# Cutting the rows of a kernel's first load into four 1 KB runs: sum of ReLU over the last axis

## The chip, the cores and the metric

One core of a Trainium2 chip; its loads are issued by SyncE (SP), whose queue runs on 16 DMA engines. The metric is the device time in microseconds (us) of one execution, the median of several. All runs quoted here were fast, with a granted clock of 1.0.

## The reference

```python
def setup_inputs():
    batch, seq, dim = 32, 512, 1024
    return {"x": np.random.randn(batch, seq, dim).astype(np.float32)}

def reference(x):
    return np.sum(np.maximum(x, 0), axis=-1).astype(np.float32)
```

16384 rows of 4 KB, 67.1 MB to read, 64 KB to write.

## The kernel before

Each of the 128 partitions takes 112 neighbouring rows of a first region and 16 of a second. The first region comes in seven chunks of 16 rows into three buffers that are used in turn; the second in ever smaller loads, so that little is left to compute when the last bytes land. ScalarE (ACT) applies ReLU in place and VectorE (DVE) sums; towards the end both do both in one instruction with an accumulator.

```python
BIG = 16; NB = 3; D = 1024
CHUNKS = [[(0, 0, 1), (0, 1, 15)]] + [[(0, 16 * c, 16)] for c in range(1, 7)]
# ... (cut)
for c in range(NBIG + 1):
    if c >= NB:
        sp.wait_ge(s_dve, done[c - NB])          # the buffer is free again
    if c < NBIG:
        i = 0
        for g, j, n in CHUNKS[c]:                # region, first row, rows
            sp.dma_start(
                out=buf[:, c % NB, i : i + n, :], in_=xv[g][:, j : j + n, :]
            ).then_inc(s_in[c], 16)
            i += n
            if c == 0:                           # issue ahead of the start barrier
                code.insert(arrival, code.pop())
                arrival += 1
# ... (cut: tail loads; compute; the last store waits for both engines)
```

The first chunk goes as two loads: one row for each partition (512 KB), then the other 15 (7.5 MB). Everything that computes on it waits for both (`s_in[0]` at 32).

## Time and profile before

| | before |
|---|---|
| time, three runs | 160.84, 160.88, 160.95 us |
| span of the profiled execution | 159.5 us |
| packets of the load queue, share of 16 engines | 2448, 98.1% |
| issue of the first load (the instruction on SP that starts it) | 0.000 to 0.383 us |
| first packet starts / last data packet ends | 1.007 / 157.107 us |

A packet is one descriptor's transfer: one contiguous run moved by one of the 16 DMA engines. The trace has start, duration and size of each; where I speak of packet records, I counted in those. "In flight" is the number of packets that have started and not ended, 16 when every engine works on one. The views that carry the argument stand in the prediction below. One line is added here, the first of the chain in order of time (start, duration, what): the issue of the first load.

```profile
0.00 0.38 SPq L91
```

### The profile page before, as it was taken

Reading aid. Unit: us, or ns where it says so; the run is one execution under the profiler, and the core shown is the slowest. Engines: PE = TensorE matmul, PEld = TensorE weight load, DVE = VectorE, ACT = ScalarE, POOL = GpSimd, SP = SyncE. Lnnn points to the kernel's source line nnn. Section 1 sums busy time; section 2 is a strip of 40 time slices with the busy share of each in tenths; the row PEclk is TensorE's granted clock in tenths of the full one; section 3 lists DMA queues with packets and bytes.
Section 4 is the critical chain, followed back from the end, with each engine's and each line's share of the span. In section 5 each row is a group of like instructions: output and inputs, shape, how many; then the busy total and the mean of one; then the engine's idle time right before and its main releaser. Section 6 shows DMA issues by size and latency. Waiting matters only on the chain.

```text
span 159.5 us, 149 instructions
## 1 busy us (share of the span) xinstructions
DVE 120.5 (76%) x59; ACT 101.5 (64%) x54; POOL 0.2 (0%) x4
## 2 busy tenths in 40 slices
DVE  0000000009999999999999999999999999898985
ACT  3000059990699808996099951999329980496975
POOL 0000000000000000000000000000000000000000
DMA  9969996996997998979969969969969979798994
GB/s 378 493 293 447 493 526 263 526 526 263 526 477 312 526 427 362 526 312 477 526 296 493 526 263 526 526 263 526 526 263 526 460 329 526 320 468 374 415 403 142
DMA packets 2449, 67.18 MB, mean 421 GB/s; under 512 B 528, under 2 KB 784, under 8 KB 1168
## 3 DMA queue, kind: packets, MB, share of 16 engines
q1 hardware_dynamic: 2448, 67.18, 98.1%
q14 instruction: 1, 0.01, 0.0%
HBM read 67.11 MB, written 0.07 MB: 421 GB/s over the span
## 4 chain that ended last, share of the span: by engine, by line
DVE 55%; DMA 34%; ACT 9%; SPq 2%; issue 0%
DVE res L156 54%; DMA buf<-in_x_dram 34%; ACT buf L141 9%; SPq L101 1%; SPq L112 1%; DVE buf L126 0%; DVE seam L126 0%; SPq L91 0%
## 5 line engine op out<-in xcount | busy, mean ns | idle before, releaser
L156 DVE TENSOR_REDUCE res<-buf 128x4 f32<-128x4096 f32 (+3 forms) x19 | 99.5, 5308 | 35.6 <-ACT buf L141 35.6
L141 ACT ACTIVATE buf<-buf 128x7168 f32<-128x7168 f32 (+5 forms) x13 | 80.4, 6233 | 46.2 <-DMA buf<-in_x_dram 46.2
L123 ACT ACTIVATE buf<-buf 128x1024 f32<-128x1024 f32 (+2 forms) x19 | 18.9, 998 | 8.9 <-DMA buf<-in_x_dram 8.9
L126 DVE TENSOR_SCALAR_CACHE_REDUCE buf<-buf 128x1024 f32<-128x1024 f32 (+2 forms) x19 | 20.7, 1142 | 1.9 <-DMA buf<-in_x_dram 1.9
L123 ACT ACTIVATION_READ_ACCUMULATOR buf<-buf 128x1 f32 x19 | 3.5, 187 | 0.0
L141 ACT ACT_TABLE_LOAD x1 | 1.3, 1283 | 1.3 <-PEq L216 1.3
L126 DVE DVE_READ_ACCUMULATOR buf<-buf 128x1 f32 x19 | 1.6, 82 | 0.0
L126 DVE TENSOR_SCALAR_CACHE_REDUCE seam<-seam 128x258 f32<-128x258 f32 x1 | 0.4, 423 | 0.0
L123 ACT ACTIVATE seam<-seam 128x130 f32<-128x130 f32 x1 | 0.3, 312 | 0.1
L123 ACT ACTIVATION_READ_ACCUMULATOR seam<-seam 128x1 f32 x1 | 0.2, 186 | 0.0
L216 POOL MEMSET const-bfloat16-1.0<- 128x1 bf16 x1 | 0.1, 101 | 0.0
L216 POOL MEMSET const-uint8-127<- 128x1 uint8 x1 | 0.1, 101 | 0.0
L216 POOL MEMSET const-float32-0.0<- 128x1 f32 x1 | 0.1, 98 | 0.2 <-issue 0.2
L216 POOL MEMSET const-float32-1.0<- 128x1 f32 x1 | 0.1, 98 | 0.0
L126 DVE DVE_READ_ACCUMULATOR seam<-seam 128x1 f32 x1 | 0.1, 83 | 0.0
## 6 DMA issues: line engine op xcount, KB each, us to landing
buf<-in_x_dram SPq DMA_DIRECT2D x1, 7680.0 KB, 21.3
buf<-in_x_dram SPq DMA_DIRECT2D x1, 4096.0 KB, 25.5
buf<-in_x_dram SPq DMA_DIRECT2D x1, 2048.0 KB, 30.0
buf<-in_x_dram SPq DMA_DIRECT2D x1, 1024.0 KB, 32.1
buf<-in_x_dram SPq DMA_DIRECT2D x1, 512.0 KB, 3.6
buf<-in_x_dram SPq DMA_DIRECT2D x1, 448.0 KB, 32.7
buf<-in_x_dram SPq DMA_DIRECT2D x1, 256.0 KB, 32.9
seam<-in_x_dram SPq DMA_DIRECT2D x1, 192.0 KB, 32.7
```

Source lines behind the costliest of these rows:

```text
L101: sp.dma_start(out=buf[:, tb, r : r + n, :], in_=xv[-1][:, r : r + n, :]).then_inc(s_in[NBIG + i], 16)
L112: sp.dma_start(out=flat[:, lo:hi], in_=rows[:, lo:hi]).then_inc(s_in[NBIG + len(TAIL) + k], 16)
L123: return act.activation(t, t, AF.Relu, accum_out=acc)
L126: return dve.tensor_scalar(out=t, in0=t, scalar1=0.0, scalar2=None, op0=ALU.max, op1=ALU.add, accum_out=acc)
L141: act.activation(t, t, AF.Relu).then_inc(s_act, 1)
L156: dve.tensor_reduce(out=res[:, c * BIG + r : c * BIG + r + n], in_=buf[:, c % NB, r : r + n, :], axis=X, op=ALU.add,).then_inc(s_dve, 1)
L216: nc = _bacc.Bacc("TRN2", target_bir_lowering=False, num_devices=1)
```

## The change

The intent: hand the first bytes over in smaller pieces, so that the engines get going sooner. The first load still takes one row of each partition, but as four runs of 1 KB, each with a descriptor of its own. To say so, the loads of the first region are written by flat columns; that changes no other access. The piece of a partition is then given as a number of runs times a length instead of one length.

```diff
-CHUNKS = [[(0, 0, 1), (0, 1, 15)]] + [[(0, 16 * c, 16)] for c in range(1, 7)]
+CHUNKS = [[(0, D), (D, BIG * D)]] + [[(16 * c * D, 16 * (c + 1) * D)] for c in range(1, 7)]
...
+    bulk = xv[0].rearrange("p j d -> p (j d)")
+    flat3 = buf[:, :, :, :].rearrange("p n j d -> p n (j d)")
...
-            i = 0
-            for g, j, n in CHUNKS[c]:
+            for lo, hi in CHUNKS[c]:
+                at = lo - BIG * D * c
                 sp.dma_start(
-                    out=buf[:, c % NB, i : i + n, :], in_=xv[g][:, j : j + n, :]
+                    out=flat3[:, c % NB, at : at + hi - lo],
+                    in_=bulk[:, lo:hi],
+                    max_dma_last_dim=D if hi == D else None,   # in bytes: runs of 1 KB
                 ).then_inc(s_in[c], 16)
-                i += n
```

## The prediction

> **What bounds the kernel now.** I read the page first, then the chain that ended last in order of time, then the waits of the issuing queue, then the single packet records of the trace. The page of the kernel before:
>
> ```profile
> span 159.5 us, 149 instructions
> DVE 120.5 (76%) x59; ACT 101.5 (64%) x54; POOL 0.2 (0%) x4
> ...
> DMA  9969996996997998979969969969969979798994
> ...
> q1 hardware_dynamic: 2448, 67.18, 98.1%
> ...
> buf<-in_x_dram SPq DMA_DIRECT2D x1, 512.0 KB, 3.6
> ```
>
> The two compute engines are busy 76% and 64% of the span. The packets of the one load queue took 98.1% of what 16 engines have in 159.5 us, that is 156.5 us for each engine. (The sixes in the DMA row are no idle time: a packet of 64 KB is booked in the slice in which it starts.) The last line is the load that the change touches: 512 KB, one row of 4 KB for each of 128 partitions, landed 3.6 us after its issue.
>
> The chain confirms the reading at the end of the kernel, where it counts, although it calls DVE 55% of the whole:
>
> ```profile
> 0.43 21.29 DMA buf<-in_x_dram
> ...
> 21.74 13.87 ACT buf L141
> ...
> 35.63 86.39 DVE res L156 x16
> ...
> 124.33 32.76 DMA buf<-in_x_dram
> 157.09 0.02 issue
> 157.12 0.44 DVE buf L126 x2
> 157.56 0.02 issue
> 157.58 0.43 DVE seam L126 x2
> ```
>
> The stretch of 86.39 us on DVE is followed by a load that takes 32.76 us from issue to landing. That load carries 128 KB; it took so long because it stood behind everything else in the queue. So DVE did not set the end, the queue did. The waits of the issuing queue say the same:
>
> ```profile
> SPq L91 <- DVE res L156: 101.5, 4, 50.7
> SPq L118 <- DMA buf<-in_x_dram: 31.8, 1, 31.8
> ```
>
> L91 waits for DVE to give a buffer back, but each time well before the queue runs dry: the first load that waits for a buffer was issued at 53.0 us, while the load ahead of it landed at 59.9 to 60.4 us, so the engines still had 7 us of packets in hand.
>
> From the packet records I counted how many packets were in flight at each moment. The first starts at 1.007 us. Sixteen are in flight, one for each engine, from 1.75 us to 157.0 us; the last data packet ends at 157.107 us. The kernel is therefore: 1.0 us until the first packet, 156.1 us of packets on every engine without a hole, and 2.4 us (159.52 - 157.11) for the last partial sums and their store. Whatever makes the packets of the first load take longer or shorter moves all after it by the same amount.
>
> **What one packet costs.** Durations of the load packets by size, from the same records:
>
> ```
> bytes    count  median ns   mean ns
> 61440     128     2267       2267
> 16384     128      611        612
>  4096     128      159        229
>  2048     128       84         85
>  1024     128       46         46
> ```
>
> The difference of the first and the third line gives (2267 - 159) / (61440 - 4096) = 0.0368 ns a byte, 27.2 GB/s for one engine and 435 for sixteen; what is left of 159 ns is 8.4 ns, a fixed cost for each packet. The 1 KB packets of the end (8 on each engine) took the 46 ns that this line gives (37.6 + 8.4).
>
> The 4 KB packets are the only size with a mean far over its median: those are the packets of the first load, and the first two or three on each engine took 224 to 867 ns. The excess is 128 x (229 - 159) = 8970 ns, 0.56 us for each engine. The view of the DMA queue from 1.00 to 2.73 us shows this start-up:
>
> ```profile
> DMA packets 107, 0.44 MB, mean 253 GB/s; under 512 B 0, under 2 KB 0, under 8 KB 107
> ```
>
> 253 GB/s where the span as a whole has 421. By 2.05 us only 108 of the 512 KB had been moved; after that every packet took 159 ns. The big second load began on the engines at 2.74 to 3.25 us, on average 3.00.
>
> **What the Trainium skill says.** "DMA: Bandwidth & Descriptors", section "Why small descriptors are slow (HBM only)", names a fixed overhead of about 3 cycles for each packet, and 32 bytes of descriptor on the fabric. The trace agrees in kind: 8.4 ns a packet. The same page, "Specifications", gives a first-byte latency of about 0.6 us for loads issued from SP and says that line rate needs 512 B or more. Here the first packet started 0.62 us after the first issue ended (0.383 to 1.007 us), and 1 KB packets ran at 22 GB/s an engine (1024 B / 46 ns) against 25.8 at 4 KB, so 1 KB is safe but not free. In "Why a DMA increments its semaphore by 16 and not by 1" it says that the slowest dimension sets the number of engines and that one descriptor moves one contiguous run. Partitions stay outermost, so I expect 16 engines still, and 512 packets in place of 128, 32 on each engine.
>
> **The change part by part.** It removes 128 packets of 4 KB and adds 512 of 1 KB; the same 512 KB go to the same places. The order of instructions on DVE, ACT and POOL does not change, nor do buffers, semaphores and waits; the second load is only written by flat columns, with the same 61440 B for each partition.
>
> - Fixed cost: 24 more packets on each engine x 8.4 ns = 0.20 us (32 x 46 = 1.47 us against 8 x 159 = 1.27). This lies on the path, since the queue never rests.
> - Part of it is hidden: until 2.05 us the engines wait for data rather than move it. 108 of 512 KB, a fifth, fall in that time, so I count four fifths: 0.16 us.
> - The start-up excess of 0.56 us: I take it for the wait for the first data[...], since an engine whose first packet took 807 ns went on at once with 159 ns. A wait for data does not depend on how it is cut. Change 0. A smaller first packet could be passed on sooner, up to 159 - 46 = 0.11 us; I count a third of that, -0.04 us.
> - The issue of the first load may take longer than 383 ns. Its successor's packets are needed from 2.74 us, and with 0.62 us from issue to packet they were there at about 1.5 us: over 1.2 us of slack. 0.
>
> Sum: +0.16 - 0.04 = +0.12 us, 161.0 us.
>
> **The rivals.**
>
> 1. *The start-up gets shorter.* If the slow first packets come from each engine taking in one 4 KB piece before it starts on the next, quarter pieces remove much of it. For it: the loss is all in the first two or three packets, and somebody cut this load off from the big one to begin with. Against it: some 4 KB packets took 156 to 159 ns as early as 1.28 us, so the size alone makes none slow. At best all 0.56 us go and 0.20 come: -0.36, 160.5 us.
> 2. *The writing of descriptors becomes the bound.* At the end of the kernel loads of 128 descriptors follow each other on SP every 0.485 us. If all of that were per descriptor it would be 3.8 ns each, and 512 would take 1.94 us: the first load would then last from 1.0 to about 3.0 us plus the first wait, and the big one would start 0.1 to 0.5 us late: 161.0 to 161.4 us. Against the cost being so high: the last store's 128 packets of 64 B started within 0.19 us, 1.5 ns each, so 512 would be written in 0.77 us (both are estimates from those spacings). If runs within a row cost more than rows, this could reach 1 us.
> 3. *The shift is swallowed somewhere.* Only a hole in the queue could do that, and there is none; what is left is the skew between the engines (0.5 us at the start of the big load, 0.26 us between the packets that end last), which could eat or add a tenth: 160.9 us.
>
> **Range and chances.** The three runs before lie within 0.11 us, so noise is small beside the terms. Rival 1 in part puts the low end at 160.6, rival 2 in its stronger form the high end at 161.4. No reading that I have reaches 2% (3.2 us): the whole first load occupies an engine for only 2 us. Chance of faster by over 2% 0.005, within 2% 0.985, slower 0.01, for descriptor writing far slower than the spacings tell.
>
> **What would show it.** About 384 more packets in the queue (2832), 512 of them new at 1 KB, 46 ns each once running; the big load starting on the engines at a mean near 3.1 us instead of 3.0; 16 packets in flight from there to the end; the last data packet 0.1 us later than 157.11 and still 2.4 us before the end. If the 1 KB packets have gaps between them, rival 2 holds; if the big load starts before 2.9 us, rival 1. A first packet that starts much later than 1.0 us, or fewer than 16 engines in use, would prove me wrong outright.

## The result, and the profile after

161.33 us (161.21 to 161.46, 6 runs) against 160.91 us (160.82 to 160.99, 6 runs): ratio 1.0026, 95% interval 1.0014 to 1.0039. A ratio here is the mean time of one kernel's fast runs over that of the other's fast runs of the same rounds, so not quite the ratio of the medians. Where I give a difference in us below, it is that of the plain means of all fast runs for the two, so it can differ from what the ratio says by up to 0.07 us (e6).

The changed kernel ran twice more beside other experiments. The three blocks:

| block | changed | before | difference of means |
|---|---|---|---|
| first | 161.33 us | 160.91 us | +0.42 us |
| again (e5) | 161.24 us | 161.04 us | +0.18 us |
| third (e10) | 161.34 us | 161.03 us | +0.21 us |

Each interval is about 0.2 us to either side, so the change costs some 0.27 us (the plain mean of the three), not the 0.42 us of the first block alone.

The page of the changed kernel, the lines that answer to those of before:

```profile
span 160.0 us, 149 instructions
DVE 120.5 (75%) x59; ACT 101.5 (63%) x54; POOL 0.2 (0%) x4
...
DMA  9969996997997989979969969969969969898993
...
q1 hardware_dynamic: 2832, 67.18, 97.9%
...
buf<-in_x_dram SPq DMA_DIRECT2D x1, 512.0 KB, 4.0
```

384 packets more, the same bytes, the same compute, and a first load that lands 0.4 us later. The chain in order of time:

```profile
0.00 0.44 SPq L93
0.44 0.05 issue
0.49 21.70 DMA buf<-in_x_dram
...
124.85 32.68 DMA buf<-in_x_dram
157.53 0.02 issue
157.56 0.44 DVE buf L129 x2
158.00 0.02 issue
158.02 0.43 DVE seam L129 x2
```

The same pieces in the same order, all of them later: the last sum (over the seam, a small buffer for the last columns and partial sums) starts at 158.02 us instead of 157.58, and the first piece, the issue, already takes 0.44 us instead of 0.38. So the time is lost at the beginning and carried to the end.

Where at the beginning, the stretches of half a microsecond show (columns: from:to, length, busy time of DVE, ACT and POOL, clock, DMA share, GB/s; packets are booked where they start). The kernel before:

```profile
1.00:1.50 0.50, 0.00 (x0) 0.24 (x1) 0.00 (x0) 1.00 1.14 156
1.50:2.00 0.50, 0.00 (x0) 0.50 (x1) 0.00 (x0) 1.00 0.75 172
2.00:2.50 0.50, 0.00 (x0) 0.50 (x1) 0.00 (x0) 1.00 0.94 377
```

The changed kernel:

```profile
1.00:1.50 0.50, 0.00 (x0) 0.12 (x1) 0.00 (x0) 1.00 0.75 84
1.50:2.00 0.50, 0.00 (x0) 0.50 (x1) 0.00 (x0) 1.00 0.56 135
2.00:2.50 0.50, 0.00 (x0) 0.50 (x1) 0.00 (x0) 1.00 0.90 305
```

The smaller pieces did not get the engines going sooner; in each stretch less was started. Single profiles differ, so here are all that bear on it, four with one run of 4 KB (before, e1, e4, e11) against three with four runs (the changed kernel, e5, e10): 115 to 156 GB/s against 74 to 102 in the first stretch, 164 to 221 against 113 to 135 in the second; in the third they overlap (319 to 377, 293 to 332). The packet records say the same in packets in flight, and e1, which has the packets of before, shows how much of it is the profile:

```
us       1.2  1.4  1.6  1.8  2.0  2.2  2.4
before    13   12   14   16   16   17   16
e1         8   11   12   13   16   17   17
changed    4    8    8   12   14   14   17
```

For the start I compare four profiles whose first load is the row in one 4 KB run (before, e1, e4, e11) with three of the changed kernel (its first, e5, e10). Mean values, in us for one engine; "idle" is the mean start of the big second load less the time of the first load's packets:

| | one run of 4 KB | four runs of 1 KB | difference |
|---|---|---|---|
| issue of the first load | 0.378 to 0.383 | 0.433 to 0.436 | +0.05 |
| first packet starts | 1.006 to 1.022 | 1.098 to 1.107 | +0.09 |
| packets of the first load | 1.78 | 1.86 | +0.08 |
| of this at full rate (8 x 159 ns, 32 x 46 ns) | 1.27 | 1.47 | +0.20 |
| of this waiting within packets | 0.51 | 0.39 | -0.12 |
| idle until the big load starts | 1.24 | 1.35 | +0.10 |
| big load starts, mean | 3.03 | 3.21 | +0.18 |

One way to read the table is two costs of about equal size: packets, of which the start-up swallowed more than half, and a later first packet. The clear parts are the first packet and the start of the big load; for the other rows the single profiles of the two groups nearly meet or overlap (packets 1.71 to 1.85 against 1.84 to 1.89, idle 1.17 to 1.33 against 1.31 to 1.37), and how the 0.18 us divides is not shown (see e2 and e3).

### The profile page after: what moved, and what is told of

The parts are those of the page before. It is cut to its first block, busy times and chain, and to the rows that moved or that the text cites. A ratio compares the mean times of both kernels' runs of the same rounds, so it can differ in the third digit from the quotient of the medians.

```text
span 160.0 us, 149 instructions
## 1 busy us (share of the span) xinstructions
DVE 120.5 (75%) x59; ACT 101.5 (63%) x54; POOL 0.2 (0%) x4
## 3 DMA queue, kind: packets, MB, share of 16 engines
q1 hardware_dynamic: 2832, 67.18, 97.9%
## 4 chain that ended last, share of the span: by engine, by line
DVE 55%; DMA 34%; ACT 9%; SPq 2%; issue 0%
DVE res L159 54%; DMA buf<-in_x_dram 34%; ACT buf L144 9%; SPq L104 1%; SPq L115 1%; DVE buf L129 0%; SPq L93 0%; DVE seam L129 0%
```

## The experiments

Before e1 to e4 three theories stood side by side, A, B and C in the expectation of e2. The theory that e5 to e11 test was made after those four: a second dimension in the issue makes the first packet start about 0.08 us late, and each packet more costs 7 to 9 ns of an engine; nothing else happened. The rivals: packets alone; a cost special to 1 KB or to the start; the writing of descriptors as the bound.

**e1: the row in one run, all else as changed.**

```diff
-                    max_dma_last_dim=D if hi == D else None,
+                    max_dma_last_dim=None,
```

> The changed code with the row left in one run of 4 KB: 128 packets again, loads still written by flat columns. Theory (all of the change's 0.42 us comes from the 1 KB runs): time of before, 160.9 us, first packet at 1.0 us, issue 383 ns, big load starting at a mean of 3.0 us. Rival (the flat views or the code around cost something): between 161.0 and 161.3 us.

Measured 161.10 us against 161.07, ratio 1.0001 (0.9987 to 1.0014); 2448 packets, issue 383 ns, first packet at 1.022 us. The flat views cost nothing that these runs resolve; the runs are the change.

**e2 and e3: two runs of 2 KB, eight of 512 B.**

```diff
-                    max_dma_last_dim=D if hi == D else None,
+                    max_dma_last_dim=2 * D if hi == D else None,    # e3: D // 2
```

> Two runs of 2 KB: 256 packets, 16 on each engine. Theory A (cost grows with the number of packets or descriptors): a third of the change's 0.42 us, so +0.14 us, 161.05 us, issue about 400 ns, first packet at about 1.04 us. Theory B (only the 8.4 ns a packet counts): +0.07 us, 160.98 us. Theory C (having a second dimension at all costs a fixed 0.2 us of issue and idle engines, and packets 8.4 ns on top): +0.27 us, 161.2 us, issue 436 ns and first packet at 1.1 us as with four runs.

> Eight runs of 512 B: 1024 packets, 64 on each engine, 56 more than before. Theory A (grows with the number): 7/3 of 0.42, +1.0 us, 161.9 us. Theory B (8.4 ns a packet alone): +0.47 us, 161.4 us. Theory C (fixed 0.2 us and 8.4 ns a packet): +0.67 us, 161.6 us. If writing descriptors becomes the bound at some 3.8 ns each (1024 take 3.9 us, while 512 KB at full rate take 1.3), the big load starts past 4.5 us and the time is over 162.4 us, with idle engines between packets.

Two runs: 161.12 us, +0.07 us, ratio 1.0005 (0.9992 to 1.0017). Eight: 161.41 us, +0.37 us, ratio 1.0023 (1.0011 to 1.0036). Eight runs cost less than any of the three theories had it (+1.0, +0.47 and +0.67 us; B is nearest and within the interval), and nothing like a bound by the writing of descriptors. The issue took 428 and 423 ns and the first packet came at 1.073 and 1.096 us: this delay came with the second dimension and hardly grew with the number of descriptors, as theory C had it. What theory C had wrong is the rest: for eight runs, 0.09 us of delay leave 0.28 us for 56 packets, 5 ns each (2 to 9 within the interval). Between 2.3 and 2.9 us a packet of 512 B started on each engine every 24 ns (340 KB a microsecond on sixteen engines) although each took 27: they overlap. Less 18.8 ns for the bytes at the prediction's 0.0368 ns each, this leaves 5 ns too.

One thing does not fit the theory: the big load started at a mean of 3.27 us with two runs, 3.20 to 3.23 with four and 3.20 with eight, so its start did not grow with the number of packets. That would suit a fixed cost of the second dimension of some 0.2 us, with the packets hidden in the start-up; the times (+0.07 us for two runs, +0.37 for eight) speak for packets. With one profile each for e2 and e3, and 0.2 us to either side of the times, the division between the two costs stays open.

**e4: 1 KB runs for a whole chunk in full swing.**

```diff
-                    max_dma_last_dim=D if hi == D else None,
+                    max_dma_last_dim=D if c == 4 else None,
```

> First load in one run; instead the whole fifth big load (8 MB, issued about 9 us ahead of its turn) in 8192 runs of 1 KB. It has 512 packets on each engine instead of 8 of 64 KB: the cost of a packet in full swing, 21 times the change's number. Theory (8.4 ns a packet and nothing else): 512 x 46 ns = 23.6 us instead of 19.4, +4.2 us, 165.1 us, 16 packets in flight throughout. Rival (writing descriptors is the bound, at 3.8 ns each 31 us for the load): holes between packets, fewer than 16 in flight, +6 us or more, and the next load's issue held up.

Measured 165.79 us, +4.73 us, ratio 1.0294 (1.028 to 1.0308). The view of the DMA queue from 82 to 100 us (busy tenths in 40 slices, then the totals), with nothing but 1 KB packets on the engines:

```profile
DMA  9999999999999999999999999999999999999999
...
DMA packets 6117, 6.26 MB, mean 348 GB/s; under 512 B 0, under 2 KB 6117, under 8 KB 6117
```

The engines had no hole (17.6 packets in flight), so descriptors came fast enough. The first engine's share of the load before this one landed at 79.43 us, of this one at 103.51: 24.08 us for 512 packets on each engine, 47.0 ns a packet, where the kernel before needs 19.36 us from one chunk to the next. 4.73 us for 504 packets more is 9.4 ns each, a little over the 8.4 ns of the prediction. The issues of the chunks on SP (duration min/median/max) show something else:

```profile
L93 SPq DMA_DIRECT2D buf<-in_x_dram x3: 328/383/10326, 70.5 to 105.0; - x3
```

The issue after this load, at 87.7 us, took 10.3 us, until about 98 us: SP was held up by what was still queued (how much, e8 shows). It cost no time here, because the engines had packets until 103.5 us.

**e5: the changed kernel again.** No edit.

> The changed kernel once more, beside others of the same chip, since +0.42 us is out of line with +0.07 us for two runs and +0.37 us for eight, and each interval is 0.2 us wide to either side. Theory (first packet 0.08 us late because of the second dimension in the issue, plus 24 packets an engine at 7 to 9 ns): +0.25 to +0.3 us. Rival (1 KB is worse than 512 B for some reason of its own): +0.4 us again.

161.24 us, +0.18 us, ratio 1.001 (0.9996 to 1.0023). The rival that 1 KB is worse than 512 B has no support.

**e6: no small first load.**

```diff
-CHUNKS = [[(0, D), (D, BIG * D)]] + ...
+CHUNKS = [[(0, BIG * D)]] + ...
-                    max_dma_last_dim=D if hi == D else None,
+                    max_dma_last_dim=None,
```

> No small first load at all: one load of 64 KB for each partition. 8 packets fewer on each engine (-0.06 to -0.08 us). Theory (the start-up excess is the wait for the first data and does not depend on how the load is cut): 0.0 to -0.1 us against before. Rival (big first packets make the start slower, which is why the row was cut off): +0.2 us or more, the first packets' durations over 2418 ns by more than 0.56 us on average.

161.10 us, +0.04 us, ratio 0.9998 (0.9985 to 1.0012; runs of 160.85 to 161.31). The first packet on each engine now moved 64 KB and took 2902 to 3713 ns, on average 3092, against 2418 for all later ones: an excess of 0.67 us an engine in one packet, where the kernel before had 0.56 us spread over two or three. The start-up loss is there however the load is cut. The expected gain of 0.06 to 0.08 us for 8 packets less was not seen; it is below what these runs resolve.

**e7: a smaller first load in a single run.** 1 KB for each partition first, then 63 KB.

```diff
-CHUNKS = [[(0, D), (D, BIG * D)]] + ...
+CHUNKS = [[(0, D // 4), (D // 4, BIG * D)]] + ...
-                    max_dma_last_dim=D if hi == D else None,
+                    max_dma_last_dim=None,
```

> The first load takes one run of 1 KB for each partition (128 packets of 1 KB instead of 4 KB), the second the other 63 KB: as many packets as before, no second dimension in the issue. Theory (cut does not matter, packets and issue do): 0.0 us against before, first packet at 1.0 us. Rival (a smaller first packet shortens the start-up): -0.1 to -0.4 us, the start-up excess well below 0.56 us an engine. Third (the small load is over before the big one's descriptors are there, at about 1.5 us): +0.1 us or more, with engines idle around 1.5 us.

161.38 us, +0.33 us, ratio 1.002 (1.0006 to 1.0034): the third expectation. Packet sizes and counts are those of a good start, the issue has one dimension (373 ns), the first packet comes at 1.009 us; but the 1 KB packets had all ended by 1.76 us, while those of the second load started at 1.51 to 2.22 us. In flight:

```
us       1.2  1.4  1.6  1.8  2.0  2.2
before    13   12   14   16   16   17
e7        15   14    9    9   10   15
```

So the first load has a use after all, or rather two kinds of start are good: one load that is large enough, or one large load alone (e6). A first load that is too short leaves the engines without work until the second's packets begin.

**e8: four rows in 16 runs of 1 KB at the start.**

```diff
-CHUNKS = [[(0, D), (D, BIG * D)]] + ...
+CHUNKS = [[(0, 4 * D), (4 * D, BIG * D)]] + ...
-                    max_dma_last_dim=D if hi == D else None,
+                    max_dma_last_dim=D if hi == 4 * D else None,
```

> The first load takes four rows in 16 runs of 1 KB (2048 packets, 128 on each engine), the second twelve rows: 120 packets an engine more than before, at the start. Theory (0.08 us once and 7 to 9.4 ns a packet): +0.9 to +1.2 us. Rival (a cost that belongs to the start alone, 0.3 us or so, and packets nearly free): below +0.7 us. Writing descriptors as the bound (3.8 ns each, 7.8 us against 5.0 at full rate): +2.5 us or more and engines idle between packets.

162.18 us, +1.10 us, ratio 1.0068 (1.0056 to 1.0081), inside what the theory said: (1.10 - 0.09) / 120 = 8.4 ns a packet. The rivals (below 0.7, above 2.5 us) are out. The issues of the chunks, with the longest one the second:

```profile
L93 SPq DMA_DIRECT2D buf<-in_x_dram x8: 327/328/2071, 0.0 to 106.0; - x8
```

The second issue ran from 0.481 to 2.552 us, held up behind 2048 descriptors; if those were written by then, it was at 1.25 ns each or less, not the 3.8 ns of the prediction's second rival (an estimate from these times). What ended the hold-up the packet records let one count: when the issue was done, 1777 of the 1 KB packets had not started. When e4's issue of 10.3 us was done, it was 1752, and in e11, where the issue behind the 1 KB load took 7.2 us, 1742. So an issue was held up until some 110 packets an engine were left ahead of it; this fits a queue with room for about that many, and not a slow writing of descriptors.

**e9: the second dimension in the issue, without more packets.** The first chunk as one load of two runs of 32 KB.

```diff
-CHUNKS = [[(0, D), (D, BIG * D)]] + ...
+CHUNKS = [[(0, BIG * D)]] + ...
-                    max_dma_last_dim=D if hi == D else None,
+                    max_dma_last_dim=32 * D if c == 0 else None,
```

> The first chunk as one load of two runs of 32 KB for each partition: 16 packets an engine for the chunk, as before (8 of 4 KB and 8 of 60 KB), but the issue has the second dimension. It takes the term of the issue alone. Theory (a second dimension makes the first packet start about 0.08 us late, and all after it with it): issue about 430 ns, first packet at about 1.08 to 1.10 us, +0.08 us against before and against the load without a split. Rival (the issue costs nothing, all of the change's cost is packets): first packet at 1.0 us, 0.0 us.

The time, 161.08 us, +0.07 us, ratio 1.0004 (0.9992 to 1.0017), is where the theory put it, but the interval holds 0 as well: that the delay costs time is argued from the chain, not measured here. The trace is clear on the delay. The issues of the chunks; the longest is the first:

```profile
L93 SPq DMA_DIRECT2D buf<-in_x_dram x7: 327/328/427, 0.0 to 105.1; - x7
```

The first packet came at 1.072 us. Among twelve profiles beside that of before, those with one dimension in the first issue have the first packet at 1.006 to 1.024 us, those with two at 1.072 to 1.107 us, from 2 runs a partition to 16.

**e10: the changed kernel a third time.** No edit.

> The changed kernel a third time, to narrow its size: +0.42 and +0.18 us so far. Theory (0.08 us and 24 packets at 8.4 ns): +0.28 us, with first packet at 1.10 us and big load at a mean of 3.2 us. Rival (my sum on record): +0.12 us.

161.34 us, +0.21 us, ratio 1.0013 (1.0000 to 1.0025): between theory and my sum, and it decides nothing between them. First packet at 1.098, big load at a mean of 3.20 us.

**e11: the four rows of e8, but in the fourth chunk.**

```diff
+CHUNKS[3] = [(48 * D, 52 * D), (52 * D, 64 * D)]
-                    max_dma_last_dim=D if hi == D else None,
+                    max_dma_last_dim=D if hi == 52 * D else None,
```

> First load in one run of 4 KB; instead four rows of the fourth chunk go as 16 runs of 1 KB, 128 packets an engine more than before, in full swing. Counterpart of the same four rows at the start, which gave +1.10 us for 120 packets. Theory (a packet costs the same anywhere, 8.4 to 9.4 ns, nothing of it hidden by the start-up): +1.1 to +1.2 us. Rival (the start is dearer by itself): +0.8 us or less here.

162.29 us, +1.25 us, ratio 1.0077 (1.0064 to 1.0091): 9.8 ns for each of 128 packets, close to e4's 9.4. At that price e8's 120 packets and its later first packet would have cost 1.17 + 0.09 = 1.26 us; they cost 1.10. The start is not dearer than the middle, rather a little cheaper. That fits the 0.12 us of waiting that vanished in the table above, but a difference of 0.16 us between two measurements with 0.2 us each does not show it by itself. The spacing of the records tells a little more: on each engine a 1 KB packet started every 43 ns in e8 from 3 to 5 us and every 47.3 from 5 to 7; in e11, every 44.9 from 61 to 63 us and every 46.9 from 63 to 65. So it is rather the beginning of a stretch of small packets that is cheaper, wherever it stands.

No version beat the kernel before. All eleven gave correct results.

## Why the prediction was right

The time, 161.0 us in 160.6 to 161.4, held 161.33; the mean cost of three blocks, 0.27 us, is a little over twice the 0.12 us of the sum. That the range held it was in part luck: its high end came from rival 2, which the runs speak against, and not from the term that was missing. Point by point:

- **The queue is the bound, and a delay at the start is carried through.** Right. The last data packet ends at 157.57, 157.51 and 157.37 us in the changed kernel (157.11 and 157.18 in before and e1), and the rest still takes 2.39 to 2.42 us.
- **384 more packets, 46 ns each.** Right: 2832 packets, median 46 ns. In full swing a packet costs 9.4 to 9.8 ns instead of 8.4 (e4, e11), so the fixed cost of 24 is 0.20 to 0.24 us.
- **What the start-up hides.** I counted -0.04 us for packets that fall into it and -0.04 us for smaller first pieces. The two cannot be told apart in the records; together they came to -0.12 us by the table (waiting within packets 0.44 to 0.58 us against 0.36 to 0.42). "A wait for data does not depend on how it is cut" was too strong: the waiting within packets was 0.39, 0.51 and 0.67 us with packets of 1, 4 and 64 KB.
- **"The issue of the first load may take longer than 383 ns. [...] 0."** This is the term that failed. I asked only whether the second load would still be in time. It was; but the first load's own packets come after its issue too, and every engine waits for those. The issue took 53 ns longer and the first packet came 0.09 us later. With this term the sum would have been 0.12 + 0.09 = 0.21 us. ("A first packet that starts much later than 1.0 us" was a sign of being wrong; 1.10 is that sign in small.)
- **Rival 1, a shorter start-up:** wrong in the form that would have paid. Less waiting within packets, but more idle time ahead of them; e6 shows the loss with packets of 64 KB too.
- **Rival 2, the writing of descriptors:** not the bound (e3, e4, e8). Its sign, gaps between the 1 KB packets, did show before 2.2 us, so the sign was no good: by 2.0 us, 288 packets of 512 B had started in e3, but 95 to 107 of 1 KB in the changed kernel.
- **Rival 3:** nothing was swallowed.
- **The mean start of the big load "near 3.1 us".** It was 3.21 us.
- **Small misreadings that carry nothing.** The records show 16 in flight until 156.8, not 157.0 us; three of the 4 KB packets after 2.05 us took 215 to 248 ns, not 159; the last store's packets started within 0.20 us; and since the records do not name engines, what one engine's second packet took is a guess.

A remainder is only partly explained: the start gives +0.18 us, the time went up by 0.27. From the big load on, the packets' own durations add up to 154.26 to 154.28 us an engine in the three profiles of the changed kernel and 154.20 in before and e1, with the same bytes: +0.07 us, for which I have no cause. Besides, in the profiled executions the slowest engine began the big load at 3.43 to 3.60 us instead of 3.25 to 3.46, and the end waits for all sixteen; whether the slow one at the start is the slow one at the end, the trace does not tell, since it does not name the engine of a packet. Why the 1 KB packets are further apart on the engines before 2.2 us is not settled either: descriptors that arrive late and data that arrive late look the same there. The counts speak for the data: by 2.0 us 40 packets of 4 KB had started in the kernel before, 49 of 2 KB in e2, 95 to 107 of 1 KB and 288 of 512 B, that is 95 to 160 KB; the counts differ sevenfold, the bytes by less than two.

## What to carry to other kernels

In a kernel that a load queue without holes sets, price a finer cut of a load as packets on each engine times the fixed cost read from the trace (here 8 to 10 ns for 1 KB in full swing), plus the delay of the first packet, and expect little from the start-up: its waiting was there with packets of 1, 4 and 64 KB. When a transfer stands first on the critical path, ask when its own first packet comes, not only whether its successor is in time. A cost of 0.2 us in 161 needs several blocks of runs: one block said 0.42, two others 0.2.

## What the Trainium skill lacked or had wrong

- "DMA: Bandwidth & Descriptors", section "Specifications", gives 512 B as the least transfer for line rate. Here 1 KB packets in full swing moved 348 GB/s (e4), 64 KB packets 433 GB/s (8 MB in 19.36 us): 1 KB is 20% below.
- The same page, "Why small descriptors are slow (HBM only)", gives the fixed cost as about 3 cycles and no clock beside it. "Advanced Engine Details and Errata", section "Clock Domains", has the clock, 850 MHz for the DMA engines, and 42 to 43 ns for an unobstructed descriptor of 1 KB. Three such cycles are 3.5 ns (an estimate from the two pages). The runs show more: 46 ns for a packet of 1 KB (median), 47.0 ns in full swing (e4), and 9.4 to 9.8 ns for each packet more (e4, e11).
- No page says that a second dimension in an issue from SP costs something: an issue of 423 to 436 ns instead of 373 to 383, and a first packet 0.05 to 0.1 us later, for 2 to 16 runs a partition.
- "DMA: Bandwidth & Descriptors" has the first-byte latency (0.6 us; here 0.62 to 0.64 from the end of the issue to the first packet, 0.64 to 0.67 with a second dimension), but not that an engine then loses another 0.4 to 0.7 us before packets run at full rate in the first load of a kernel: 0.39 us with packets of 1 KB, 0.51 with 4 KB, 0.67 with 64 KB (e6).
- No page says how far an issuing queue runs ahead. "Perfetto Trace Analysis", section "DMA Instruction — HWDGE (DVE, Sync)", has a descriptor buffer that can fill, but no size. Here an issue behind 2048 queued descriptors took 2.07 us (e8) and one behind a load of 8192 took 10.3 us (e4); they and a third (7.2 us, e11) were done when 1742 to 1777 packets were left to start, some 110 an engine.
